# A two-layer streaming encoder step: two chunks of the first mixer's output read back in pieces through the ring of weight staging tiles

## The chip, the core and the metric

One core of one Trainium2 chip runs the whole program. The time is device microseconds of one launch. TensorE (PE, with its weight loads PEld), VectorE (DVE), ScalarE (ACT) and GpSimd (POOL) compute; SyncE (SP) only issues transfers, most of them on one hardware queue, in the order of the program. POOL issues the others, on a software queue.

## What is computed

Two layers on a prompt of 1024 frames and 8 streams of 16 frames (1152 tokens, width 1024). The part around the change is layer 0's mixer: stick-breaking attention (8 heads, in 4 pairs) beside a Conformer convolution, both joined and projected.

```python
def ab_mixer_prompt(h, w_in, w_out, dw_w, dw_b, ln_g, ln_b):
    q, k, v, u = ab_project(h, w_in)
    a_out = stick_breaking(q, k, v, ...)               # 512 columns: 4 pairs of heads
    c_out = conv_module(u_ext, dw_w, dw_b, ln_g, ln_b) # 512 columns
    out = jnp.concatenate([a_out, c_out], axis=-1) @ w_out
```

`x + out` then goes through an MLP, and so does layer 1 after its own attention.

## The kernel before, in words

Activations stand with channels on the 128 partitions: a chunk is 128 channels by 1152 tokens, and 1152 tokens are three groups `g` of `G` = 384. Products in full precision are done with every operand split into a high part and a rest (`split`, L182: ACT writes the high part at L185, DVE the rest at L186), three products each (`dense`, L211, matmuls at L225).

`mixer0` (L655) runs pair after pair, `p` = 0 to 3. While pair `p` attends (scores `z` L924 to L927, sigmoids L928 and L929, a running product on DVE L907 and L909, transposes `tpa` L388, products `ava` L398, result `cpa` L410), the projection of pair `p + 1` (`psp`) fills PE, and DVE does the taps of the convolution (`y`, `u`, L735). The samples' attention (`zs` L568, from cache tiles `ct`, which have 3 buffers) is merged in. `merge` and `level` set the order by given costs; a step's `after` and `lag` hold it back. Behind that, a scheduler places each engine's instructions, and every engine keeps that order.

The outputs of the pairs 0, 1 and 2 go to the scratch tensor `cat_d` in HBM (`cat_d<-cpa`, L363, on POOL's queue), because the tiles for them are those of the mixer's input `h`, which is read until the last projection. In the last pair (`p` = 3) the output projection starts with the three chunks that are done: `part_out` (L1069) multiplies chunks 0 to 2 by the weights `wo0a0` to `wo0a7`, into `psoa`. To that end `ready_chunks` (L1056) reads a chunk back into one tile `cr` of 128x1152 (its place is that of `sk`, the keys of the pair; there is one) and splits it into `cat` in three pieces. The names: `cr00` and `cr01` are chunks 0 and 1, `cr02` is chunk 2, which comes later; `cat0_00` and `cat0_01` are the high part and the rest of chunk 0, `cat0_10` and `cat0_11` of chunk 1. `expand` (L344) reads `sk` a last time at L351.

Weights come in through `staging` (L190): three tiles `st` of 128x512 in a ring; the split of one, on ACT and DVE, writes one of four tiles `hl` and gives the `st` tile free for the next transfer. A step's staged transfers come in the order in which the program asks for them.

```python
if p == 3:
    late, = ready_chunks(0, [2], pp, cat_t)
    late.name, late.after, late.lag = "ready", carry[-1].name, 3000.0
    fill[0].after, fill[0].lag = "ready", 5000.0
    fill = ready_chunks(0, range(2), pp, cat_t) + first + [late] + fill
```

Of the kernel before, what the change touches and what calls it, by code (L numbers as in the profile page):

```python
# [21 lines left out]
G = 384  # L22
NG = 3
# [17 lines left out]
def f(ap):  # L41
    return ap.bitcast(F32)
# [56 lines left out]
def run(steps):  # L99
    for s in steps:  # L100
        s.go()
# [23 lines left out]
def tile_trunk(ctx, tc, ins, outs):  # L125
# [8 lines left out]
    def pool(name):  # L134
        return tc.tile_pool(name=name, bufs=1, reuse_waits="tile")
# [7 lines left out]
    def bank(name):  # L143
        return psum.tile([P, 512], F32, tag="ps", name=name)
# [31 lines left out]
    cat_d = [dram.tile([KC, P, T], F32, name=f"cat_d{l}") for l in range(2)]  # L176
# [6 lines left out]
    def split(hi, lo, src):  # L183

        ACT(hi, src, AF.Copy)  # L185
        return tt(lo, src, f(hi), ALU.subtract)  # L186
# [3 lines left out]
    def staging(src, name, n=512):  # L190
        st = sp.tile([P, 512], F32, tag="st", name=f"st_{name}")
        dma(st[:, :n], src)
        return st
# [54 lines left out]
    chunks = {}  # L248
# [5 lines left out]
    def new_hs(name):  # L254
        return [[new_h(g, half, name) for half in range(2)] for g in range(NG)]
# [365 lines left out]
    def two_samples(a, b):  # L621

        (ka, sa, ta, pa), (kb, sb, tb, pb) = a, b
        if len(ta) == 1:
            return ka + sa + kb + ta + sb + pa + tb + pb
        return ka + sa + kb + ta[:1] + pa[:1] + ta[1:] + sb + pa[1:] + tb[:1] + pb[:1] + tb[1:] + pb[1:]
# [17 lines left out]
    def pipeline(jobs, carry):  # L644


        steps = []
        for first, second, tail in jobs:
            h = (len(carry) + 1) // 2
            steps += [first] + carry[:h] + [second] + carry[h:]  # L650
            carry = tail
        return steps, carry


    def mixer0():  # L655
        with ExitStack() as st:
# [8 lines left out]
            pp = Bufs(st.enter_context(pool("pair0")))  # L665
# [77 lines left out]
            def ag(c):  # L743
                return (chunk_steps(at[16 + c], got, ahead, h, ks, lambda ps, g: gate(c, ps, g), f"g{c}")
                        + chunk_steps(at[12 + c], got, ahead, h, ks, lambda ps, g: value(c, ps, g), f"a{c}"))
# [124 lines left out]
            def proj(p):  # L870
                steps = []
                for n, tag in enumerate(("sq", "sk", "sv")):
                    def evac(ps, g, n=n, tag=tag):
                        if g == 0:
                            S[tag, p] = pp.tile([P, T], F32, tag, f"{tag}0{p}")
                        if g < 2:
                            tt(S[tag, p][:, g * G:g * G + G], ps[:, :G], rstd[g], ALU.mult)
                        else:
                            ACT(S[tag, p][:, g * G:], ps[:, :G], AF.Copy)
                        if g == 2 and n:  # L880
                            put(outs["sb_k" if n == 1 else "sb_v"][p], S[tag, p])
                    steps += chunk_steps(at[4 * n + p], got, ahead, h, ks, evac, f"p{p}{n}")
                return steps

            def expand_qk(p):
                q, k = S["sq", p], S["sk", p]
                expand(qs, kd, kl, q, k)
                S["qn"] = pp.tile([P, P], F32, "qn", f"qn0{p}")
                S["kn"] = pp.tile([P, P], F32, "kn", f"kn0{p}")
                ACT(S["qn"], q[:, TP:], AF.Copy, scale=0.125)  # L890
                ACT(S["kn"], k[:, TP:], AF.Copy)
# [73 lines left out]
            carry, cat_t = [], None  # L965
            for p in range(4):
                S["p"] = p
                expand_qk(p)
                if p < 3:
                    fill = proj(p + 1)  # L970
                    if p < 2:
                        fill[10:10] = ag(p + 2)
                    n = TAPS[p + 1]
                    mix, now, taps = [], taps[:n], taps[n:]
                else:
                    cat_t = new_hs("cat0")
                    (first, fill), now = part_out(0, range(3), pp, cat_t), []
                    for s in taps:
                        s.pe = 900.0
                    mix = taps + conv_norm(lambda: (conv_pool.close(), Bufs(st.enter_context(pool("ln")), t1=3, yl=5))[1],  # L980
                                           cat_t)
                cat = Cat(0, p, wk, cat_t)
                jobs = attend(p, cat)
                body, left = pipeline(jobs[1:], jobs[0][2])
                steps = carry + [jobs[0][0]] + [Step(327.0, lambda p=p, g=g: expand_v(p, g)) for g in range(NG)]
                if p == 3:
                    late, = ready_chunks(0, [2], pp, cat_t)
                    late.name, late.after, late.lag = "ready", carry[-1].name, 3000.0
                    fill[0].after, fill[0].lag = "ready", 5000.0
                    fill = ready_chunks(0, range(2), pp, cat_t) + first + [late] + fill  # L990
                steps += [jobs[0][1]] + body
                carry = left
                if p == 3:
                    steps += carry
                cs = sample_out(cat, wk, p)
                load = sample_caches(0, p, cp)
                sample = two_samples(*(sample_steps(0, p, bg, S, wk, load, soft, cs) for bg in range(2)))
                run(level(merge(steps, sample, fill, mix), now))
            return cat_t

    def conv_norm(new_pool, cat_t):

        steps = []

        pools = []

        def norm(g):
            box = {}

            def load():  # L1010
                if g == 0:
                    pools.append(new_pool())
                box["y"] = [pools[0].tile([P, G], F32, "yl", f"yl{g}{c}") for c in range(4)]
                for c in range(4):
                    put(box["y"][c], cat_d[0][4 + c, :, g * G:g * G + G])

            def centre():
                yl = box["y"]
                mu = bank(f"mu{g}")
                for c in range(4):  # L1020
                    mm(mu[:, :G], ones, yl[c], start=c == 0, stop=c == 3)
                for c in range(4):
                    stt(yl[c], mu[:, :G], -1.0 / 512, yl[c], ALU.mult, ALU.add)

            def squares():
                yl, box["acc"] = box["y"], None
                for c in range(4):
                    box["acc"] = add_square(box["acc"], yl[c], pools[0], f"l{g}{c}")

            def scale():  # L1030
                box["r"] = pools[0].tile([P, G], F32, "r", f"rl{g}")
                diag, box["rows"], _ = rstd_of(box["r"], pools[0], box["acc"], 1.0 / 512, LN_EPS, f"l{g}")
                diag(box["acc"])

            def out(c):
                y = box["y"][c]
                tt(y, y, box["r"], ALU.mult)
                s = pools[0].tile([P, G], F32, "t1", f"ls{g}{c}")
                gg, bb = cvec[:, 1, c:c + 1], cvec[:, 2, c:c + 1]
                ACT(s, y, AF.Sigmoid, bias=bb, scale=gg)  # L1040
                ACT(y, y, AF.Identity, bias=bb, scale=gg)
                tt(y, y, s, ALU.mult)
                split(cat_t[g][1][0][:, c, :], cat_t[g][1][1][:, c, :], y)

            name = f"ln{g}"
            return ([Step(50.0, load, 0.0, f"l{name}"),
                     Step(2600.0, centre, 1900.0, f"c{name}", f"l{name}", 4000), Step(500.0, squares, 1400.0),
                     Step(700.0, scale, 1200.0, f"s{name}", f"c{name}", 5000),
                     Step(800.0, lambda: box["rows"](), 0.0, None, f"s{name}", 2500)]
                    + [Step(300.0, lambda c=c: out(c), 1500.0) for c in range(4)])  # L1050

        for g in range(NG):
            steps += norm(g)
        return steps

    def ready_chunks(layer, chunks, pp, cat_t):  # L1056

        steps = []
        for c in chunks:
            def go(c=c):  # L1060
                cr = pp.tile([P, T], F32, "sk", f"cr{layer}{c}")
                dma(cr, cat_d[layer][c])
                for g in range(NG):
                    hi, lo = (x[:, c % 4, :] for x in cat_t[g][c // 4])
                    split(hi, lo, cr[:, g * G:g * G + G])
            steps.append(Step(300.0, go))
        return steps
# [899 lines left out]
```

## Time and profile before

| what | value |
|---|---|
| median of 3 runs | 2749.17 us (2747.8 to 2751.32) |
| the profiled execution | 2750.03 us |
| its span, first to last instruction | 2748.2 us |
| PE busy | 2669.0 us (97%) |
| DVE busy | 2090.5 us (76%) |
| mean granted clock of PE | 0.991 |
| transfers of `cr` (10 in the program), issue to landing | 3.7 / 4.8 / 7.9 us (min, median, max) |
| the last pair of the first mixer, 425 to 548 us | PE busy 109.09 of 123.00 us |

The span is the program on the chip; the execution's time has 1.8 us more around it. A table like this tells which engine is full on the average; what one stage is worth is read in its own stretch of the trace, by what each engine waited for there.

### The profile page before, as it was taken

The page shows a single profiled execution, that of the slowest core. Times are in us where ns is not written, and L with a number is a line of the kernel's source. Part 1 is how long each engine was busy: PE and PEld are TensorE (multiplying, and loading weights), DVE is VectorE, ACT ScalarE, POOL GpSimd, SP SyncE. Part 2 cuts the span into 40 slices and gives each one's busy share as a digit, 9 for nine tenths or more (in the row PEclk, how much of TensorE's full clock was granted, in tenths as well). Part 3 has the DMA queues.
Part 4 walks back from the last instruction along what each step waited for, and adds up shares of the span by engine and source line. Part 5 has one row for each costly group of instructions (what it writes and reads, how often), then busy time and mean ns, then how long its engine had stood idle before and what let it go on. Part 6 is the DMA issues. An engine that isn't in the chain of part 4 may idle for free.

```text
span 2748.2 us, 50583 instructions
## 1 busy us (share of the span) xinstructions
PE 2669.0 (97%) x19362; PEld 2557.1 (93%) x19362; DVE 2090.5 (76%) x4117; ACT 1389.0 (51%) x2906; POOL 328.3 (12%) x599
## 2 busy tenths in 40 slices
PE   8999898999999999999999999998999999999998
PEld 8987776799999999999999999997999999999998
DVE  8999998888777755758577777778787777647577
ACT  5344456755554543435355555556555555434344
POOL 1100101041111100000011111110221111100001
PEclk9999999999999999999999999999999999999999
DMA  4434446454343377435444444446533343684344
GB/s 157 121 111 147 118 141 223 145 176 143 139 146 141 138 260 250 124 100 170 146 140 138 140 135 135 139 132 229 179 132 137 141 145 138 230 270 134 96 125 145
DMA packets 173203, 422.90 MB, mean 154 GB/s; under 512 B 25968, under 2 KB 53808, under 8 KB 170912
## 3 DMA queue, kind: packets, MB, share of 16 engines
q1 hardware_dynamic: 135696, 288.38, 33.1%
q0 software_dynamic: 37120, 131.27, 13.9%
q8 instruction: 152, 2.49, 0.4%
q14 instruction: 91, 0.75, 0.1%
q10 hardware_dynamic: 144, 0.02, 0.0%
HBM read 289.60 MB, written 117.34 MB: 148 GB/s over the span
## 4 chain that ended last, share of the span: by engine, by line
PE 76%; DVE 12%; ACT 4%; issue 4%; DMA 3%; POOL 0%; SPq 0%; DVEq 0%; ACTq 0%; POOLq 0%
PE um L1461 25%; PE pd L1686 25%; PE psc L225 10%; PE psp L225 3%; DVE y L735 3%; PE avc L467 2%; PE tpc L455 2%; DVE kp L907 2%; PE f L225 1%; PE psoa L225 1%; DMA cr<-cat_d 1%; PE zc L1201 1%; PE zc L1202 1%; PE zs L568 1%; PE so L602 1%
## 5 line engine op out<-in xcount | busy, mean ns | idle before, releaser
L225 PE MATMUL psc<-h,hl_wc 128*128 128x384 f32 x1728 | 327.2, 339 | 0.0
L225 PEld LDWEIGHTS psc<-h,hl_wc 128*128 128x128 f32 x1728 | 296.8, 188 | 13.3 <-issue 10.9
L1461 PE MATMUL um<-sl,hl_m 128*128 128x288 f32 x1548 | 240.3, 295 | 0.0
L1461 PEld LDWEIGHTS um<-sl,hl_m 128*128 128x128 f32 x1548 | 217.7, 188 | 0.0
L1686 PE MATMUL pd<-tm,hl_wd 128*128 128x288 f32 x1584 | 214.7, 294 | 0.0
L1686 PEld LDWEIGHTS pd<-tm,hl_wd 128*128 128x128 f32 x1584 | 211.3, 189 | 0.0
L735 DVE SCALAR_TENSOR_TENSOR y<-u,dw,y 128x1024 f32<-128x1024 f32 (+1 forms) x232 | 177.8, 806 | 0.6
L225 PE MATMUL psp<-h,hl_wi 128*128 128x384 f32 x864 | 165.7, 344 | 0.0
L1468 ACT ACTIVATE hdm<-hdm 128x288 f32<-128x288 f32 x192 | 84.7, 442 | 156.5 <-DVE hdm L1467 154.8
L225 PEld LDWEIGHTS psp<-h,hl_wi 128*128 128x128 f32 x864 | 150.9, 191 | 7.0 <-issue 6.2
L186 DVE TENSOR_TENSOR tm<-xr,tm 128x576 fp32r<-128x576 f32 (+1 forms) x120 | 85.8, 715 | 93.9 <-ACT tm L185 93.6
L185 ACT ACTIVATE tm<-xr 128x576 fp32r<-128x576 f32 (+1 forms) x120 | 77.6, 646 | 95.8 <-PE pd L1686 74.0
L1168 ACT ACTIVATE s<-s,mxc 128x640 f32<-128x640 f32 (+4 forms) x128 | 88.9, 694 | 60.2 <-DVE mxc L1165 58.6
L1461 PE MATMUL um<-sl,hl 128*128 128x288 f32 x756 | 119.1, 296 | 0.0
L1686 PE MATMUL pd<-th,hl_wd 128*128 128x288 f32 x792 | 113.7, 297 | 3.8 <-DVE th L186 3.7
L1686 PEld LDWEIGHTS pd<-th,hl_wd 128*128 128x128 f32 x792 | 108.2, 190 | 4.8 <-DVE th L186 4.2
L1686 PE MATMUL pd<-xr,hl_wd 128*128 128x288 f32 x792 | 112.4, 296 | 0.0
L1686 PEld LDWEIGHTS pd<-xr,hl_wd 128*128 128x128 f32 x792 | 108.0, 190 | 0.0
L1461 PEld LDWEIGHTS um<-sl,hl 128*128 128x128 f32 x756 | 106.4, 188 | 0.8
L1686 PE MATMUL pd<-tm,hl 128*128 128x288 f32 x768 | 104.9, 295 | 0.0
L1686 PEld LDWEIGHTS pd<-tm,hl 128*128 128x128 f32 x768 | 103.1, 188 | 0.0
L185 ACT ACTIVATE whc<-tpc 128x512 fp32r<-128x512 f32 (+1 forms) x144 | 72.5, 523 | 46.7 <-PE tpc L455 45.8
(526 smaller groups left out, 6637.0 us busy)
## 6 DMA issues: line engine op xcount, KB each, us to landing
xr<-hb_d SPq DMA_DIRECT2D x208, 288.0 KB, 3.0
xr<-in_w_up_dram SPq DMA_DIRECT2D x64, 512.0 KB, 4.2
hb_d<-hdm POOLq DMA_DIRECT2D x96, 288.0 KB, 2.4
hb_d<-t POOLq DMA_DIRECT2D x96, 288.0 KB, 2.4
wm<-in_w_down_dram SPq DMA_DIRECT2D x64, 256.0 KB, 4.0
st_wd<-in_w_down_dram SPq DMA_DIRECT2D x64, 256.0 KB, 3.5
st_wc<-in_w_in_c_dram SPq DMA_DIRECT2D x44, 256.0 KB, 2.9
xm_d<-xo POOLq DMA_DIRECT2D x16, 576.0 KB, 3.5
```

The lines of the kernel that those rows point to most:

```text
L185: ACT(hi, src, AF.Copy)
L186: return tt(lo, src, f(hi), ALU.subtract)
L225: mm(ps()[:, :G], hl[:, a, at:at + P], act[g][k // 4][b][:, k % 4, :], start=n == 0, stop=n == len(todo) - 1)
L455: nc.tensor.transpose(tp[:, c0 + q * P:c0 + (q + 1) * P], blocks.get(j, tile_q), ident)
L467: mm(st["av"][:, o0:o0 + n], vs[:, j, i].rearrange("p a d -> p (a d)"), src[:, c0:c0 + n], start=st["done"] == 0, stop=st["done"] == nmm - 1)
L568: mm(box["z"][at // 512][own, at % 512:at % 512 + kw], qb[:, own], k[:, b * kw:b * kw + kw], start=True, stop=True)
L735: stt(src if j == CW - 1 else dst, src, wj, dst, ALU.mult, ALU.add)
L907: nc.vector.tensor_tensor_scan(keep[:, 0:n][:, ::-1], keep[:, 0:n][:, ::-1], ones[:, 0:1].to_broadcast([P, n]), 1.0, ALU.mult, ALU.mult)
L1168: ACT(s[:, :n], s[:, :n], AF.Exp, bias=mx, scale=-1.0, accum_out=tot)
L1461: mm(banks[b, n][:, :TQ], w[:, a, c * P:c * P + P], combo(key, c)[:, h, n * TQ:n * TQ + TQ], start=k < 3 and c == 0 and i == 0, stop=c == ...
L1468: ACT(y, y, AF.Relu)
L1686: mm(ps, w[:, a, m * P:m * P + P], b[:, h, (n - ns[0]) * TQ:(n - ns[0]) * TQ + TQ], start=first and s == 0, stop=j == NJ - 1 and s == 2, s ...
```

## The change

Chunks 0 and 1 are no longer read whole into `cr`. A new function asks for each in three pieces of 128x384, each into a staging tile `st` (named `st_cr000` to `st_cr002` for chunk 0, `st_cr010` to `st_cr012` for chunk 1), and splits the piece from there. Chunk 2 comes as before. The calls stand at the same place of the program, ahead of the first weights of the output projection. Lines behind it are numbered 8 higher.

```diff
-                    fill = ready_chunks(0, range(2), pp, cat_t) + first + [late] + fill
+                    fill = ready_pieces(0, range(2), cat_t) + first + [late] + fill
...
+    def ready_pieces(layer, chunks, cat_t):
+
+        def go(c, g):
+            st = staging(cat_d[layer][c, :, g * G:g * G + G], f"cr{layer}{c}{g}", G)
+            split(*(x[:, c % 4, :] for x in cat_t[g][c // 4]), st[:, :G])
+
+        return [Step(100.0, lambda c=c, g=g: go(c, g)) for c in chunks for g in range(NG)]
```

How it moves instructions. SP's queue, from the last transfer that both have at the same place to the fourth tile of the last pair's sample keys (`ct03k03`), before:

```order
L537 DMA ct03k02_4520<-in_sb_k_dram 128x4x256
L1062 DMA cr00_4450<-cat_d0_109 128x1152
L1079 DMA xo00_4703<-in_x_dram 128x3x384
L192 DMA st_wo0a5_0_5125<-in_w_out_ab_dram 128x384
L192 DMA st_wo0a6_0_5297<-in_w_out_ab_dram 128x384
L1062 DMA cr01_4467<-cat_d0_109 128x1152
L537 DMA ct03k03_4533<-in_sb_k_dram 128x4x256
```

and with the change (`xo00` is the residual of the first output chunk):

```order
L1087 DMA xo00_4711<-in_x_dram 128x3x384
L192 DMA st_cr010_4471<-cat_d0_109 128x384
L192 DMA st_cr011_4477<-cat_d0_109 128x384
L192 DMA st_cr012_4481<-cat_d0_109 128x384
L192 DMA st_wo0a0_0_4485<-in_w_out_ab_dram 128x384
L192 DMA st_wo0a1_0_4490<-in_w_out_ab_dram 128x384
L192 DMA st_wo0a2_0_4730<-in_w_out_ab_dram 128x384
L192 DMA st_wo0a3_0_4820<-in_w_out_ab_dram 128x384
L192 DMA st_wo0a4_0_5000<-in_w_out_ab_dram 128x384
L192 DMA st_wo0a5_0_5133<-in_w_out_ab_dram 128x384
L192 DMA st_wo0a6_0_5305<-in_w_out_ab_dram 128x384
L537 DMA ct03k03_4541<-in_sb_k_dram 128x4x256
```

The three pieces of chunk 0 have taken the places that `wo0a0`, `wo0a1` and `wo0a2` had, far ahead of this stretch; the pieces of chunk 1 and seven weights now stand here, ahead of `ct03k03`.

DVE, from the last `cpa` of pair 2's second half to the end of the splits, before (`hl_wo0a2` and `hl_wo0a3` are weights; the splits of `hl_wo0a0` and `hl_wo0a1` stand much earlier, among the taps):

```order
L410 TENSOR_TENSOR cpa212_4417<-ava212_4408,ata212_4415 64x256
L186 TENSOR_TENSOR hl_wo0a2_0_4724<-st_wo0a2_0_4722,hl_wo0a2_0_4724 128x384
L186 TENSOR_TENSOR hl_wo0a3_0_4814<-st_wo0a3_0_4812,hl_wo0a3_0_4814 128x384
L186 TENSOR_TENSOR cat0_01_4453<-cr00_4450,cat0_00_4452 128x384 x3
L186 TENSOR_TENSOR cat0_11_4470<-cr01_4467,cat0_10_4469 128x384 x3
```

and with the change:

```order
L410 TENSOR_TENSOR cpa212_4417<-ava212_4408,ata212_4415 64x256
L186 TENSOR_TENSOR cat0_01_4439<-st_cr000_4436,cat0_00_4438 128x384
L186 TENSOR_TENSOR cat0_01_4439<-st_cr001_4456,cat0_00_4438 128x384
L186 TENSOR_TENSOR cat0_01_4439<-st_cr002_4460,cat0_00_4438 128x384
L186 TENSOR_TENSOR cat0_11_4474<-st_cr010_4471,cat0_10_4473 128x384
L186 TENSOR_TENSOR cat0_11_4474<-st_cr011_4477,cat0_10_4473 128x384
L186 TENSOR_TENSOR cat0_11_4474<-st_cr012_4481,cat0_10_4473 128x384
L186 TENSOR_TENSOR hl_wo0a0_0_4487<-st_wo0a0_0_4485,hl_wo0a0_0_4487 128x384
L186 TENSOR_TENSOR hl_wo0a1_0_4492<-st_wo0a1_0_4490,hl_wo0a1_0_4492 128x384
L186 TENSOR_TENSOR hl_wo0a2_0_4732<-st_wo0a2_0_4730,hl_wo0a2_0_4732 128x384
L186 TENSOR_TENSOR hl_wo0a3_0_4822<-st_wo0a3_0_4820,hl_wo0a3_0_4822 128x384
```

The four weights of the projection are now split behind both chunks.

PE, from the first product of the output projection (`psoa000`, first group), before (`tpa213` are transposes for the last quarter of pair 2):

```order
L225 MATMUL psoa000_4494<-cat0_00_4452,hl_wo0a0_0_4479 128x384
L388 MATMUL tpa2132_4501<-ident_69,sg216_4299 128x128
L388 MATMUL tpa2132_4501<-ident_69,sg217_4344 128x128
L388 MATMUL tpa2132_4501<-ident_69,sg216_4299 128x128
L388 MATMUL tpa2132_4501<-ident_69,sg217_4344 128x128
L225 MATMUL psoa000_4494<-cat0_01_4453,hl_wo0a0_0_4479 128x384
L225 MATMUL psoa000_4494<-cat0_00_4452,hl_wo0a0_0_4479 128x384
L388 MATMUL tpa2133_4508<-ident_69,sg216_4299 128x128
L388 MATMUL tpa2133_4508<-ident_69,sg217_4344 128x128 x2
L568 MATMUL zs0300_4514<-ct03k00_4516,qb0_124 32x256 x4
```

and with the change:

```order
L225 MATMUL psoa000_4502<-cat0_00_4438,hl_wo0a0_0_4487 128x384
L225 MATMUL psoa000_4502<-cat0_01_4439,hl_wo0a0_0_4487 128x384
L225 MATMUL psoa000_4502<-cat0_00_4438,hl_wo0a0_0_4487 128x384
L225 MATMUL psoa000_4502<-cat0_10_4473,hl_wo0a0_0_4487 128x384
L225 MATMUL psoa000_4502<-cat0_11_4474,hl_wo0a0_0_4487 128x384
L225 MATMUL psoa000_4502<-cat0_10_4473,hl_wo0a0_0_4487 128x384
L388 MATMUL tpa2132_4509<-ident_69,sg216_4299 128x128
L388 MATMUL tpa2132_4509<-ident_69,sg217_4344 128x128
L388 MATMUL tpa2132_4509<-ident_69,sg216_4299 128x128
L388 MATMUL tpa2132_4509<-ident_69,sg217_4344 128x128
L388 MATMUL tpa2133_4516<-ident_69,sg216_4299 128x128
L388 MATMUL tpa2133_4516<-ident_69,sg217_4344 128x128 x2
```

The products with chunk 1 have moved up next to those with chunk 0, and the transposes stand behind all six. What stands ahead of the first `psoa` and behind the twelfth to eighteenth is in the same order in both.

## Rows read from the trace of the kernel before

**Rows 1.** The head of the profile's page: span, and the shares of the chain that ended last.

```profile
span 2748.2 us, 50583 instructions
PE 76%; DVE 12%; ACT 4%; issue 4%; DMA 3%; POOL 0%; SPq 0%; DVEq 0%; ACTq 0%; POOLq 0%
```

**Rows 2.** The chain that ended last, in order of time, 400 to 560 us: start us, us, what.

```profile
421.99 1.54 DVE u L735 x2
423.56 1.23 DVE l L351
424.81 7.86 DMA cr<-cat_d
...
434.77 6.57 DMA cr<-cat_d
441.36 0.53 ACT cat L185
441.94 2.44 PE psoa L225 x12
...
452.08 4.01 DMA cr<-cat_d
```

**Rows 3.** PE's timeline: start us, us, engine, line, operation, tiles, shape, count, and in brackets the idle time before it with what ended it.

```profile
429.67 1.03 PE L388 MATMUL tpa<-ident,sg 128*128 128x128 f32 x6 [4.14 <-DVE sg L909]
433.27 0.69 PE L225 MATMUL psoa<-cat,hl_wo0a 128*128 128x384 f32 x1 [2.57 <-ACT cat L185]
...
438.33 2.85 PE L1021 MATMUL mu<-yl,ones 128*128 128x384 f32 x8
441.94 2.44 PE L225 MATMUL psoa<-cat,hl_wo0a 128*128 128x384 f32 x12 [0.76 <-ACT cat L185]
444.30 1.94 PE L398 MATMUL ava<-wa,vs 128*64 128x256 f32 x16
...
447.90 0.64 PE L568 MATMUL zs<-ct03k,qb 128*32 128x256 f32 x8
...
453.22 1.78 PE L225 MATMUL psoa<-cat,hl_wo0a 128*128 128x384 f32 x9
456.69 3.48 PE L225 MATMUL psoa<-cat,hl_wo0a 128*128 128x384 f32 x18 [1.68 <-ACT cat L185]
```

**Rows 4.** DVE's timeline, the same columns; the first four rows are from 380 to 400 us, the others from 408 to 470 us.

```profile
388.88 0.53 DVE L186 TENSOR_TENSOR hl_wo0a<-st_wo0a,hl_wo0a 128x384 fp32r<-128x384 f32 x1
389.33 1.35 DVE L909 TENSOR_TENSOR sgs<-sgs,kps 128x1151 f32<-128x1151 f32 x1
...
397.21 0.56 DVE L186 TENSOR_TENSOR hl_wo0a<-st_wo0a,hl_wo0a 128x384 fp32r<-128x384 f32 x1
397.69 1.21 DVE L351 TENSOR_TENSOR l<-sk,k 64x1024 fp32r<-64x1024 f32 x1
...
429.90 0.42 DVE L410 TENSOR_TENSOR cpa<-ava,ata 64x256 f32<-64x256 f32 x1
430.35 1.03 DVE L186 TENSOR_TENSOR hl_wo0a<-st_wo0a,hl_wo0a 128x384 fp32r<-128x384 f32 x2
433.25 1.50 DVE L186 TENSOR_TENSOR cat<-cr,cat 128x384 fp32r<-128x384 f32 x3 [1.87 <-ACT cat L185]
441.91 1.50 DVE L186 TENSOR_TENSOR cat<-cr,cat 128x384 fp32r<-128x384 f32 x3 [7.17 <-ACT cat L185]
```

**Rows 5.** ACT's timeline, the same columns.

```profile
418.38 0.53 ACT L185 ACTIVATE hl_wo0a<-st_wo0a 128x384 fp32r<-128x384 f32 x1 [0.54 <-PE psp L225]
419.08 1.05 ACT L348 ACTIVATE k<-sk 64x1024 fp32r<-64x1024 f32 x1 [0.17 <-PE z L924]
...
432.69 1.35 ACT L185 ACTIVATE cat<-cr 128x384 fp32r<-128x384 f32 x3 [1.84 <-DMA cr<-cat_d]
```

**Rows 6.** SP's timeline of issues: start us, us from the first to the last of the row.

```profile
366.53 0.89 SPq L192 DMA_DIRECT2D st_wo0a<-in_w_out_ab_dram  x2
...
430.94 0.86 SPq L192 DMA_DIRECT2D st_wo0a<-in_w_out_ab_dram  x2
434.77 0.33 SPq L1062 DMA_DIRECT2D cr<-cat_d  x1
437.16 11.81 SPq L537 DMA_DIRECT2D ct03k<-in_sb_k_dram  x4
```

**Rows 7.** Issue to landing. The first row is the tile view of `st_wo0a`, over its 8 transfers. The others are issues of short windows (count, KB of each, median us to landing), in this order: issued at 389 to 389.6 us, at 430.9 to 431.1 us, at 431.3 to 431.6 us, at 425.5 to 428 us, at 437 to 438 us, and the writes of `cat_d` at 401 to 422 us and at 446 to 449 us.

```profile
DMA to landing us min/median/max: 2.3/3.4/7.3
...
st_wo0a<-in_w_out_ab_dram SPq DMA_DIRECT2D x1, 192.0 KB, 3.1
...
st_wo0a<-in_w_out_ab_dram SPq DMA_DIRECT2D x1, 192.0 KB, 6.0
...
st_wo0a<-in_w_out_ab_dram SPq DMA_DIRECT2D x1, 192.0 KB, 7.3
...
xo<-in_x_dram SPq DMA_DIRECT2D x1, 576.0 KB, 10.2
...
ct03k<-in_sb_k_dram SPq DMA_DIRECT2D x1, 512.0 KB, 5.6
...
cat_d<-cpa POOLq DMA_DIRECT2D x2, 64.0 KB, 1.9
...
cat_d<-cpa POOLq DMA_DIRECT2D x1, 64.0 KB, 4.5
```

**Rows 8.** Stages: window, us, busy us (count) of PE, PEld, DVE, ACT and POOL, granted clock of PE, share and GB/s of the DMA engines.

```profile
380.00:390.00 10.00, 10.00 (x95) 8.67 (x94) 9.78 (x9) 7.15 (x19) 0.00 (x0) 1.00 0.01 2
390.00:400.00 10.00, 9.94 (x65) 8.47 (x64) 9.92 (x18) 6.26 (x15) 2.16 (x5) 1.00 0.68 236
...
430.00:433.00 3.00, 0.70 (x5) 0.30 (x3) 1.35 (x3) 0.91 (x2) 2.83 (x6) 0.54 1.03 364
433.00:436.00 3.00, 2.73 (x10) 2.25 (x10) 1.50 (x3) 2.12 (x5) 0.94 (x2) 0.50 1.07 393
436.00:442.00 6.00, 5.24 (x29) 2.34 (x28) 0.09 (x1) 1.73 (x4) 0.00 (x0) 0.91 0.99 350
```

## The prediction

> **What bounds the kernel now.** First the head of the page: PE holds 76% of the chain that ended last, transfers 3% [rows 1]. On the average there is nothing to win but PE time. The change, though, is one stretch of 20 us, so the second view is the chain by time, around 425 us [rows 2]. Up to 423.6 us DVE leads with the taps; then DVE's last read of `sk` (L351), and from 424.81 us the chain is a transfer of `cr` (7.86 us), its split, a second transfer of `cr` (6.57 us), its split, and the twelve products that waited for it. The reader sees two reads, one behind the other, through one tile.
>
> Third, PE's timeline there [rows 3]. PE waits 4.14 us for DVE's `sg`, which is not touched, then 2.57 us for chunk 0 (first `psoa` at 433.27 us) and 0.76 us for chunk 1. Between these two PE had other work: transposes, `zs`, `mu`. So what the reads cost is 3.3 us, not the 14 us that they hold of the chain. The chunk-1 wait ends at 441.94 us and `ava` starts at 444.30 us. If the first product came at a time T and nothing waited behind it, `ava` would start at T + 444.30 - 433.27 - 0.76 = T + 10.27 us. In other words: **the stretch is as long as before if T = 434.0 us** (433.27 + 0.76). Everything below is the search for T.
>
> **What the change removes, adds and moves.**
>
> *The transfers.* Two of 576 KB become six of 192 KB, four more issues on SP of some 0.4 us each [rows 6], in time in which SP waits anyway. The bytes are the same.
>
> *Chunk 0 early.* Its pieces take the places of the first three weights on SP's queue, of which two were issued at 366.53 us [rows 6]. They lie in `st` long before they are wanted. ACT can write the high part when the last projection has read `h` for the last time. It stands where the split of `wo0a2` stood, which ran at 418.38 us right after PE gave way [rows 5]. Three pieces take 1.35 us [rows 5] against 0.53 us, which delays the copy `k` at 419.08 us by some 0.5 us at most; DVE reads it at 423.56 us, so that hides it.
>
> *DVE among the taps.* Two weight splits leave it. The next instruction started 0.45 us after one and 0.48 us after the other [rows 4], in a stretch where DVE is busy 9.78 and 9.92 us of 10 [rows 8]. I take the whole 0.93 us as gained; the bounds are 0 and 0.93.
>
> *The wait that the change adds.* DVE writes chunk 0's rest only behind the last `cpa`, where before the weights' splits began at 430.35 us [rows 4]; now 429.42 us. Until then the three `st` tiles are held. Only then can the pieces of chunk 1 be asked for, and the weights `wo0a0` to `wo0a2` only when these have been split in turn. Before, the weights were in `hl` and one tile was read twice; now it is chunk 0, a round of transfers, a round of transfers, and the first product needs the second round. PE's queue keeps everything else behind that product: the transposes and `zs` that filled the time between the two waits stand behind it now.
>
> *T, step by step.* 429.42 + 0.5 (a third of the 1.50 us of three rests [rows 4]): the first `st` tile is free at 429.9 us and `cr010` is issued at 430.0. It lands after L1. From landing to the next issue: landing at 432.69, next issue at 434.77 with three pieces [rows 5, 6], so 2.08 us less two rests of 0.5, 1.06 us. `wo0a0` lands after L2. From landing to the first product: 441.36 to 441.94 [rows 2, 3], 0.58 us. T = 430.0 + L1 + 1.06 + L2 + 0.58 = 431.64 + L1 + L2. Against 434.03 the stretch is **longer by L1 + L2 - 2.39 us**.
>
> *L1 and L2.* For 192 KB the trace has 2.3 us at the least, 3.4 in the middle, 7.3 at the most [rows 7]. The two slow ones were asked for at 430.9 and 431.4 us, the very place: 6.0 and 7.3 us [rows 7]. But ahead of them on the queue stood `cr00` and `xo00`, which landed at 436.3 us (426.06 + 10.2 [rows 7]; its issue is the one behind `cr00`); they landed 0.6 and 2.4 us after that. Now `xo00` is first. I give it the 7.86 us that `cr00` took in that place [rows 2] from 425.1 us: 433.0 us. A piece 0.6 to 2.4 us behind lands at 433.6 to 435.4 us, that is L1 = 3.6 to 5.4; I take 4.2, nearer the lower end, because 576 KB less stand in the queue. For L2 I take the 3.1 us of 389 us [rows 7]: `ct03k03`, which before was asked for at 437.16 us [rows 6], is not in the queue yet. T = 438.9 us, and the stretch is longer by 7.3 - 2.39 = **4.9 us**. Bounds: 2.3 + 2.3 gives +2.2 us, 7.3 + 6.0 gives +10.9 us. No end is a gain: for that L1 + L2 would have to be under 2.39 us, and one of them alone has 2.3 us at the least.
>
> *What is queued behind.* `wo0a3` must wait for the tile of `wo0a0`: issue at T + 0.5, its high part split at T + 0.5 + 3.1 + 0.56 = T + 4.2 us. ACT's copies of the transposes stand behind it; `ava` wants them at T + 10.27 us: hidden. `ct03k03` stands behind `wo0a6`, which waits for the split of `wo0a3`: issue at T + 5.1 us, landing 5.6 us later [rows 7] at T + 10.7; PE wanted it at 447.90 us [rows 3], now T + 13.87. Covered by 3.2 us; it costs if the third round takes over 6.3 us.
>
> *The third chunk.* Its write and read (`cat_d<-cpa`, 4.5 us [rows 7], then `cr`, 4.01 us [rows 2]) hang on `ava` and shift with it; PE waits 1.68 us for it before and after [rows 3]. The write may meet less traffic, since sample keys stood beside it before; in a quiet place it took 1.9 us [rows 7]. So between 0 and 1.68 us come back; I take 0.5, near the row of the place itself.
>
> *PE's clock.* In 430 to 436 us the granted clock is 0.54 and 0.50, and 0.91 in 436 to 442: PE's low level, 1.2 of 2.4 GHz, up to some 437 us [rows 8], after the 4.14 us of waiting. So the first 3.8 us from 433.27 already run slow and lie in the 10.27 us. After T I take the same; ending earlier or later by that much gives or takes half of it, 1.9 us. The Trainium skill, "TensorE: Matmul & The Clock Gate", section "HAM oscillation — how this bites in real kernels", speaks against the change: a PE that waits for transfers is throttled and starts its next work cold. By that rule alone one would add the 1.9 us for the longer wait; by the rows nothing, since the clock is down there already.
>
> *Sum.* 4.9 - 0.5 = **+4.4 us**, and behind 460 us no engine has a source that does not shift along. The profiled execution would go from 2750.0 to 2754.4 us; the median shown is 0.86 us below that execution, so **2753.6 us** for it.
>
> **The rivals.** 0.2% of the time, 5.5 us, is about what a measurement of this kernel can tell from no change. The forecast lies just within.
>
> *Slower by more: both rounds meet a full queue.* Place: the pieces at 430 us and the weights some 5 us later. For it: the transfer share is 1.03 and 1.07 in 430 to 436 us [rows 8], and the two transfers asked for there took 6.0 and 7.3 us. Against it: 576 KB of them have left this time. With 6.0 and 4.5 us the stretch grows by 8.1 us, with the upper bounds by 10.9: 2757.3 to 2760. It decides from L1 + L2 = 8.4 us on (+6.0 less 0.5). The Trainium skill, "DMA: Bandwidth & Descriptors", section "Issuing engines are not separate DMA queues", says that what POOL asks for runs on the same engines and interleaves; the values and `yl` that POOL moves then would slow both rounds.
>
> *No change at all: short rounds and the third chunk's wait closed.* L1 + L2 = 5.5 and 1.68 us given back: +1.4 us, 2750.6 us. For it: half of the eight weight transfers took 3.4 us or less [rows 7]. Against it: those ran in quiet times.
>
> *Faster, as the change reads.* If the products did not wait for weights, PE would save 2.57 + 0.76 us and DVE's 0.93 us: -4.3 us, 2744.9 us; to pass 5.5 us the third chunk's wait must close too. Against it stands the order: the weights are asked for behind the chunks, through the same three tiles.
>
> **How the numbers follow.** Forecast 0.50, of which a fifth lies above 5.5 us; full queues 0.31; no change 0.13; faster 0.06, half of it by over 0.2%. So slower 0.10 + 0.31 = 0.41, faster 0.03, the same 0.56. The range, 2749.0 to 2759.5 us, holds the forecast with its clock term, no change, and most of the slower case; faster and the far upper end are left out. The forecast's own range is 2751 to 2756.
>
> **What would show it.** Step by step: the first `psoa` not at 433.3 but near 439 us, its wait put down to the split of `wo0a0`, some 9 us long with what DVE's part of it leaves; no wait of its own for chunk 1; `cr010` issued near 430.0 us; `cat` for chunk 0 on ACT near 418 us; `ava` near 449 us; `ct03k03` without a wait. Wrong would be: a first product before 434.5 us, weights asked for before 434 us, PE waiting for `ct03k03`, or a later stretch in which the shift is given back.

## The result, and the profile after the change

The change makes the kernel slower: 2759.03 us (median of 6 runs, 2755.76 to 2764.15) against 2751.06 us (6 runs), a ratio of 1.0032 [1.002, 1.0045], that is +8.8 us [+5.5, +12.4]; the two medians alone are 8.0 us apart. The forecast was +4.4 us, with 2753.6 us: the same direction and about half the size. Two further blocks of the unaltered change gave +8.2 us [+5.2, +11.3] and +7.2 us [+4.1, +9.9].

The profiled execution took 2764.15 us, span 2762.4 us. It already ran 4.95 us behind the first execution of the kernel before at 367 to 375 us, where both do the same. So times are best read as differences inside the stretch. PE's timeline, to be held against [rows 3]:

```profile
433.84 1.54 PE L388 MATMUL tpa<-ident,sg 128*128 128x128 f32 x6 [5.62 <-DVE sg L909]
444.18 2.29 PE L225 MATMUL psoa<-cat,hl_wo0a 128*128 128x384 f32 x6 [8.79 <-ACT hl_wo0a L185]
446.26 1.70 PE L388 MATMUL tpa<-ident,sg 128*128 128x128 f32 x7
...
450.75 2.85 PE L1021 MATMUL mu<-yl,ones 128*128 128x384 f32 x8
453.14 1.51 PE L225 MATMUL psoa<-cat,hl_wo0a 128*128 128x384 f32 x6
454.58 1.94 PE L398 MATMUL ava<-wa,vs 128*64 128x256 f32 x16
...
467.40 3.50 PE L225 MATMUL psoa<-cat,hl_wo0a 128*128 128x384 f32 x18 [1.93 <-ACT cat L185]
```

In place of two waits for chunks, 2.57 and 0.76 us, there is one, 8.79 us, and it is put down to the split of a weight. Behind it nothing waits up to `ava`. SP's issues and ACT's splits (to be held against [rows 5, 6]) show why:

```profile
430.23 0.37 SPq L1087 DMA_DIRECT2D xo<-in_x_dram  x1
435.11 1.61 SPq L192 DMA_DIRECT2D st_cr<-cat_d  x3
439.90 8.69 SPq L192 DMA_DIRECT2D st_wo0a<-in_w_out_ab_dram  x7
449.03 10.39 SPq L537 DMA_DIRECT2D ct03k<-in_sb_k_dram  x4
```

```profile
420.27 1.39 ACT L185 ACTIVATE cat<-st_cr 128x384 fp32r<-128x384 f32 x3
...
438.76 0.52 ACT L185 ACTIVATE cat<-st_cr 128x384 fp32r<-128x384 f32 x1 [2.69 <-DMA st_cr<-cat_d]
439.95 0.52 ACT L185 ACTIVATE cat<-st_cr 128x384 fp32r<-128x384 f32 x1 [0.67 <-DMA st_cr<-cat_d]
442.25 0.52 ACT L185 ACTIVATE cat<-st_cr 128x384 fp32r<-128x384 f32 x1 [1.77 <-DMA st_cr<-cat_d]
443.60 0.52 ACT L185 ACTIVATE hl_wo0a<-st_wo0a 128x384 fp32r<-128x384 f32 x1 [0.83 <-DMA st_wo0a<-in_w_out_ab_dram]
```

Two rounds one behind the other: pieces of chunk 1 asked for at 435.11, the first split at 438.76 (3.65 us), the first weight asked for at 439.90 (1.14 us later), split at 443.60 (3.70 us), first product 0.58 us after that. DVE, to be held against [rows 4]:

```profile
434.08 0.42 DVE L410 TENSOR_TENSOR cpa<-ava,ata 64x256 f32<-64x256 f32 x1
434.53 1.50 DVE L186 TENSOR_TENSOR cat<-st_cr,cat 128x384 fp32r<-128x384 f32 x3
439.32 0.56 DVE L186 TENSOR_TENSOR cat<-st_cr,cat 128x384 fp32r<-128x384 f32 x1 [3.30 <-ACT cat L185]
...
453.63 1.95 DVE L1023 SCALAR_TENSOR_TENSOR yl<-mu,yl 128x384 f32<-128x384 f32 x4 [5.40 <-PE mu L1021]
455.50 1.87 DVE L296 TENSOR_TENSOR sq_l<-sq_l,sq_l 128x384 f32<-128x384 f32 x3
457.40 0.42 DVE L410 TENSOR_TENSOR cpa<-ava,ata 64x256 f32<-64x256 f32 x1
```

The staging tiles come free with the rests at 434.53, right behind `cpa`. In the last three rows the last `cpa` of pair 2 starts the moment three `sq_l` have ended. In the kernel before it stood behind two of them and waited for ACT, with 0.36 us to spare; the third came behind it:

```profile
445.19 1.22 DVE L296 TENSOR_TENSOR sq_l<-sq_l,sq_l 128x384 f32<-128x384 f32 x2
446.77 0.42 DVE L410 TENSOR_TENSOR cpa<-ava,ata 64x256 f32<-64x256 f32 x1 [0.36 <-ACT ata L406]
447.22 0.56 DVE L296 TENSOR_TENSOR sq_l<-sq_l,sq_l 128x384 f32<-128x384 f32 x1
```

So DVE's order differs here too; the order lists above end ahead of this place. Every profile of the change has three squares ahead of that `cpa`, and both profiles of the kernel before have two.

The stages of the change, to be held against [rows 8] (columns as there):

```profile
434.00:440.00 6.00, 1.39 (x6) 0.98 (x6) 2.52 (x6) 1.76 (x4) 3.77 (x7) 0.50 1.01 327
440.00:444.00 4.00, 0.00 (x0) 0.00 (x0) 1.11 (x2) 1.40 (x3) 0.00 (x0) 0.50 0.71 256
444.00:449.00 5.00, 4.83 (x22) 3.51 (x22) 2.23 (x4) 2.59 (x6) 0.00 (x0) 0.50 0.52 156
449.00:455.00 6.00, 6.00 (x32) 3.95 (x34) 1.37 (x3) 1.33 (x3) 0.00 (x0) 1.00 0.69 204
```

The granted clock is at its low level through the wait and through the next 4.8 us of work.

**A measure for one stretch.** Below, M is the time between two writes on POOL's queue that every kernel here has: the last-but-one `cpa` of pair 2 and the last one. First the kernel before:

```profile
430.70 0.55 POOL L363 DMA_DIRECT2D cat_d<-cpa  x1
447.48 0.55 POOL L363 DMA_DIRECT2D cat_d<-cpa  x1 [13.54 <-DVE cpa L410]
```

then the change:

```profile
434.88 0.55 POOL L363 DMA_DIRECT2D cat_d<-cpa  x1
458.11 0.55 POOL L363 DMA_DIRECT2D cat_d<-cpa  x1 [20.00 <-DVE cpa L410]
```

M is 16.78 us before and 23.23 us in this execution: +6.45 us. A kernel's first write may itself come earlier; the change wins 0.78 us there (below). Each M is read from one profile. It repeats well for the kernel before (16.78 and 16.65 us) and for the change (23.23, 23.33 and 23.65 us), but one kernel below has 16.40 us in one execution and 14.48 us in another.

### The profile page after: what moved, and what is told of

It reads as the page before. It is cut to its first block, busy times and chain, and to the rows that moved or that the text cites. A ratio compares the mean times of both kernels' runs of the same rounds, so it can differ in the third digit from the quotient of the medians.

```text
span 2762.4 us, 50594 instructions
## 1 busy us (share of the span) xinstructions
PE 2674.7 (97%) x19362; PEld 2562.1 (93%) x19362; DVE 2090.9 (76%) x4117; ACT 1388.8 (50%) x2906; POOL 328.2 (12%) x599
## 4 chain that ended last, share of the span: by engine, by line
PE 70%; DVE 4%; ACT 2%; DMA 2%; issue 1%; DVEq 0%; ACTq 0%; SPq 0%
PE pd L1694 26%; PE um L1469 25%; PE psc L225 10%; PE avc L467 2%; PE tpc L455 2%; PE zc L1209 1%; PE zc L1210 1%; PE psoa L225 1%; DMA cr<-cat_d 1%; PE so L602 1%; PE zs L568 1%; DVE xr L1375 0%; PE psob L225 0%; ACT s L1176 0%; DMA xr<-in_w_up_dram 0%
```

## The experiments

Edits are against the changed kernel unless said. Theory A is the prediction's: two rounds of transfers ahead of the first product.

**The change once more.**

> The changed kernel once more, for a second profile. Measure M: from POOL's write of the last-but-one cpa of pair 2 to its write of the last one (16.8 us before, 23.2 us in the first profile of the change). Theory A (two rounds of transfers in the stretch, the rest is wander from execution to execution): M is again 22 to 24 us, the time 5 to 7 us over before, and the other shifts of the first profile (+2.1 us in the first 60 us, +1.4 at 235, +1.5 at 350, some +3.5 behind 530) come with other sizes or not at all. Theory B (the four additional issues and splits, or where the code now lies, cost time elsewhere as well): the same shifts at the same places, 8 to 14 us over before.

+8.2 us [+5.2, +11.3], M = 23.33 us. In this profile the early offset is gone (+0.47 us at 367 to 375 us in place of 4.95) and the stretch is the same, so the offset belongs to the execution and not to the change. In M and in the shifts theory A holds, and theory B's shifts at the same places did not come. The time is another matter: +8.2 us lies above theory A's 5 to 7 us, in theory B's 8 to 14, and the interval shuts out neither.

**The weights ahead of the pieces.**

```diff
-                    fill = ready_pieces(0, range(2), cat_t) + first + [late] + fill
+                    fill = first[:1] + ready_pieces(0, range(2), cat_t) + first[1:] + [late] + fill
```

> The weights wo0a0 and wo0a1 are asked for ahead of the pieces, the pieces still come through the staging tiles. Theory A (what cost time is that the weights stand behind two rounds of pieces): chunk 0 and its weights are there before PE wants them, chunk 1 takes one round which the transposes, zs and mu hide; M = 12 to 15 us, the time 3 to 6 us under before. Rival C (the pieces themselves cost: small transfers land late, four more splits): M stays over 17 us and the time at or over before.

M = 18.60 us, +1.4 us [-1.4, +4.1]: the first product does come early, but the forecast of a gain fails, and both numbers are those of rival C. PE's, SP's and ACT's timelines of this kernel:

```profile
425.67 0.42 PE L225 MATMUL psoa<-cat,hl_wo0a 128*128 128x384 f32 x1
...
438.87 0.69 PE L225 MATMUL psoa<-cat,hl_wo0a 128*128 128x384 f32 x1 [4.22 <-ACT cat L185]
```

```profile
426.95 0.44 SPq L537 DMA_DIRECT2D ct03k<-in_sb_k_dram  x1
431.35 2.21 SPq L192 DMA_DIRECT2D st_cr<-cat_d  x3
```

```profile
438.30 0.52 ACT L185 ACTIVATE cat<-st_cr 128x384 fp32r<-128x384 f32 x1 [3.00 <-DMA st_cr<-cat_d]
```

The wait has moved to chunk 1, whose first piece takes 6.95 us from issue to split (431.35 to 438.30) in place of 3.05 to 4.90 us in the change. With the weights gone from SP's queue, `ct03k03` (512 KB) is asked for ahead of it. A good part of the round that was taken out came back as a longer landing of the other. That `ct03k03` is the reason is read from the order and not tested.

**One round only: chunk 1 through `cr`.**

```diff
-                    fill = ready_pieces(0, range(2), cat_t) + first + [late] + fill
+                    fill = ready_pieces(0, [0], cat_t) + ready_chunks(0, [1], pp, cat_t) + first + [late] + fill
```

> Only chunk 0 comes in pieces; chunk 1 comes whole through the tile of sk as before. The weights still stand behind the pieces of chunk 0. Theory A: one round less than the change, so the first product comes about one landing and two splits (4 to 6 us) earlier than in the change: M = 17.5 to 19.5 us, the time 0 to 3 us over before. Rival C (pieces cost, by number): half of the excess of the change goes, M = 20.

M = 19.71 us, +3.3 us [+0.6, +6.1]: 3.6 us less than the change in M and 4.9 us in time. PE's first product:

```profile
437.46 1.01 PE L225 MATMUL psoa<-cat,hl_wo0a 128*128 128x384 f32 x2 [5.23 <-ACT hl_wo0a L185]
```

It waits 5.23 us for the weight, asked for at 431.96 us and split at 436.89. One round less, some 3.6 us less in M. But 19.71 us lies between theory A's upper end (19.5) and rival C's 20, so this run alone does not tell the two apart; the run with weights first and chunk 1 through `cr`, below, does.

**No round: chunk 0 in an idle tile** (from the kernel before; the taps' buffer is free by then, so both chunks can come early and the weights stay where they were).

```diff
-                    fill = ready_chunks(0, range(2), pp, cat_t) + first + [late] + fill
+                    early = cv.tile([P, UW], F32, "u", "cr00")[:, :T]
+                    dma(early, cat_d[0][0])
...
+                    fill = [Step(300.0, first_chunk)] + ready_chunks(0, [1], pp, cat_t) + first + [late] + fill
```

> The kernel before, but chunk 0 is read whole into a tile of the convolution that has been idle since some 320 us, so that chunk 1 need not wait for chunk 0's split; nothing goes through the staging tiles. Theory A: both waits for chunks (2.57 and 0.76 us) go, and PE can do a first product and zs while it waits 4.1 us for DVE: M = 12 to 15 us, 3 to 6 us under before. If the reads were hidden anyway: same time as before, M = 16 to 17.

M = 16.40 us, -2.2 us [-4.7, +0.6]. M is that of the expectation's other line (16 to 17 us), and a gain of 3 to 6 us isn't shown. The wait for chunk 1 did not go: chunk 1 was asked for 10 us earlier than before (424.69 us), but needed 9 us to be split (433.76), and PE still waited for it:

```profile
434.34 0.69 PE L225 MATMUL psoa<-cat,hl_wo0a 128*128 128x384 f32 x1 [2.27 <-ACT cat L185]
```

**The same a second time.**

> The kernel with chunk 0 in an idle tile, a second time: 16.40 us between the puts and -2.2 us (-4.7 to +0.5) the first time. By the stretch alone: 16 to 17 us and -1.5 to +1 us. If the first time's gain holds: -4 to -2 us.

M = 14.48 us, under the 16 to 17 us that were expected, and -0.8 us [-3.3, +1.7]. Here chunk 1 was waited for 1.02 us. The kernel's time is the lowest in both blocks, but neither block tells it from the kernel before.

**Weights first, chunk 1 through `cr`.**

```diff
+                    fill = (first[:1] + ready_pieces(0, [0], cat_t) + ready_chunks(0, [1], pp, cat_t)
+                            + first[1:] + [late] + fill)
```

> Weights first, chunk 0 in pieces through the staging tiles, chunk 1 whole through the tile of sk. Theory A (pieces cost nothing by themselves; only what stands behind them in the ring does): as e4, M = 16 to 17 us, the time 0 to 4 us under before. Rival C (pieces cost): M over 17.5.

M = 16.35 us as expected, and 0.0 us [-2.8, +2.8], the upper end of what was expected. PE's first products:

```profile
424.06 0.42 PE L225 MATMUL psoa<-cat,hl_wo0a 128*128 128x384 f32 x1
...
431.56 0.69 PE L225 MATMUL psoa<-cat,hl_wo0a 128*128 128x384 f32 x1 [0.57 <-ACT cat L185]
```

No weight is waited for, and chunk 1 costs 0.57 us of waiting. Chunk 0 through the staging tiles shows no cost, in M or in time, so long as the first product waits for no weight and chunk 1 does not come through the same tiles behind it. For chunk 0 that speaks against rival C: the one-round kernel has the same pieces and differs only in the place of the weights, and its M was 19.71 us.

**Sixteen idle products ahead of the first one** (the idle-tile kernel; PE multiplies chunk 0's high part with itself into a spare bank, 9 times ahead of the wait for `sg` and 7 times behind it, so that the first products don't meet a low clock; the results are never read).

> As e4, with 16 products of 128x384 on PE that nothing reads, between the transposes for which PE waits: they are additional work and only keep PE busy in its wait for DVE. Theory D (in e2 and e4 the waits that went were eaten by PE's low clock: it was low for 6 us of work in each): the clock is up when the output projection begins, the low stretch is under 2 us, M = 13.5 to 15 us and the time 3 to 6 us under before. Rival: the clock does not matter and chunk 1's landing at 433 us sets the end: M = 16 to 17, the time as e4.

M = 14.65 us as expected, but +4.1 us [+1.4, +6.9] in time, where a gain was expected. The second time, beside the idle tile alone:

> The kernel with chunk 0 in an idle tile and 16 idle products, a second time. The first time its stretch was 2.1 us shorter than that of the kernel before (14.65 against 16.78 us between the two puts) and its time 4.1 us longer, with a mean granted clock of 0.9899 over 12 runs against 0.9918 of the kernel before on that chip. Theory A (chance): the clock of these runs is that of the kernel before within 0.0005 and the time -3 to +1 us. Theory B (the low clock elsewhere belongs to the kernel): between the puts 14 to 15 us again, the mean clock 0.001 to 0.002 lower, the time +3 to +6 us.

M = 14.89 us and +3.3 us [+0.6, +5.8]. The mean granted clock of the runs was 0.9907 against 0.9912: within theory A's bound, while the time fits theory B. So by these numbers some 2 us are won in the stretch against the kernel before and 5 to 6 us lost outside it, twice. Both profiles fall back in several steps of 1 to 2 us behind 460 us, but single executions do so anyway: between DVE's instructions at 470 us and the last ones these two lose 4.4 and 3.4 us against the first execution of before, the kernel with the weights first, which has no idle products, loses 4.8, and the third execution of the change gains 1.2. The cause is not settled. Nor do the idle products win anything sure in M over the idle tile alone, which had 16.40 and, in this block, 14.48 us.

**The kernel before, once more.**

> The kernel before once more, for a second profile: what differs between two executions of one program. Theory A: M is 16.5 to 17.0 us again; outside of that stretch the starts differ by up to 2 us at places where PE waits, as they did between the two profiles of the change.

M = 16.65 us, one run of 2754.51 us. But the wander that the expectation allowed, 2 us, is exceeded: the execution is 1.18 us ahead of the first one at 338 us and 3.11 us behind it at 367 us (on DVE and on POOL's write). Two stages of the kernel before in each of its two profiles (columns as in [rows 8]), first the execution that the prediction read:

```profile
307.00:311.00 4.00, 4.00 (x44) 3.30 (x43) 3.94 (x6) 0.98 (x2) 0.53 (x1) 0.57 0.18 28
334.00:342.00 8.00, 5.49 (x44) 4.30 (x45) 7.86 (x11) 2.46 (x5) 1.63 (x3) 1.00 0.42 123
```

then the second:

```profile
307.00:311.00 4.00, 4.00 (x48) 3.71 (x37) 3.94 (x7) 1.14 (x4) 0.53 (x1) 1.00 0.64 197
334.00:342.00 8.00, 6.67 (x31) 6.11 (x31) 7.86 (x12) 1.47 (x3) 1.64 (x3) 0.57 0.42 108
```

The same program has its clock low at 307 us in one execution and at 334 us in the other. Such stretches move single executions by some us, which is why a stretch is judged here by M and not by where it lies.

**The change with 32 idle products**, 9 behind the first transpose and 23 behind the next three, in the two waits that PE has anyway.

```diff
+                    def warm():
+                        spare = bank("warm")
+                        hi = cat_t[0][0][0][:, 0, :]
+                        for n in range(32):
+                            mm(spare[:, :G], hi[:, :P], hi, start=True, stop=True)
...
+                    fill = (ready_pieces(0, [0], cat_t) + [Step(0.0, warm)] + ready_pieces(0, [1], cat_t)
+                            + first + [late] + fill)
```

> The change with 32 idle products (of chunk 0 with itself, into a spare bank, never read) on PE in the two waits ahead of the first product of the output projection: 9 behind the first transpose, 23 behind the next three. In the change PE does 4.5 us of work at the low clock after its first product at 439.9 us. Theory A (that work is what the low clock costs): with PE busy up to some 3 us before that product the clock is up, 2.2 us come back, and the time between the two puts of pair 2 on POOL, 23.2 to 23.3 us in the change, falls to 20.5 to 22; the time falls with it, 2 to 3 us under the change, +5 to +7 against the kernel before. Theory B (what is won in the stretch is lost at a low clock elsewhere, as the warmed kernel before this seemed to show, 2.1 us won and 4.1 lost): the same 20.5 to 22, but the time stays at the change's, +7 to +11, and the mean granted clock of the runs is no higher than the change's.

M = 20.81 us, as both theories had it, and +8.0 us [+5.0, +11.3] where the change beside it had +7.2: theory B's time. PE's timeline, then its stages:

```profile
430.46 6.21 PE L994 MATMUL warm<-cat 128*128 128x384 f32 x23
436.51 0.60 PE L388 MATMUL tpa<-ident,sg 128*128 128x128 f32 x4
439.97 0.62 PE L225 MATMUL psoa<-cat,hl_wo0a 128*128 128x384 f32 x2 [2.86 <-ACT hl_wo0a L185]
...
448.22 1.94 PE L398 MATMUL ava<-wa,vs 128*64 128x256 f32 x16
```

```profile
430.00:435.00 5.00, 5.00 (x18) 5.00 (x19) 2.03 (x5) 0.79 (x2) 3.77 (x7) 0.52 0.99 324
435.00:440.00 5.00, 2.14 (x15) 1.87 (x13) 1.72 (x4) 2.47 (x6) 0.00 (x0) 1.00 0.75 270
440.00:444.00 4.00, 4.00 (x31) 3.06 (x35) 1.88 (x4) 2.31 (x5) 0.00 (x0) 1.00 0.59 161
```

The clock is up before the first product, and from that to `ava` are 8.25 us in place of 10.33 to 10.40. So the low clock costs the change 2.1 us in its stretch. In the time the 2.1 us don't show. Against the change beside it the intervals are too wide to say that they were lost. Against the kernel before something is: up to the third chunk this execution is 2.96 us later (its offset of 1.01 us taken off), which is under the whole interval. Theory B is not met either, for its mean clock was to be no higher than the change's, and it is (0.9913; the change 0.9901, before 0.9912). Where the time goes is open; the profiled execution is the fastest of its six.

**The change a third time**, beside the last three on one chip.

> The change unaltered, beside the three others on one chip. Theory (the stretch and little more): 22.5 to 24 us between the puts, +5.5 to +9 us. Rival (more is lost behind the stretch): +9 to +12 us with the same stretch. In both the mean granted clock is 0.001 to 0.002 under that of the kernel before, since the clock is low for 17 us of the stretch and not for 6.8.

M = 23.65 us, +7.2 us [+4.1, +9.9]; mean granted clock 0.9901 against 0.9912. All three numbers are those of the theory of the stretch and little more; the interval alone does not shut out the rival's range.

## Why the prediction was right in its mechanism and too small in its size

The table takes from each profile of the change its own offset ahead of the taps (+4.95, +0.47 and -0.81 us on POOL's writes at 367 to 375 us), so that every entry is a time later than in the kernel before.

| step | forecast | first | second | third |
|---|---|---|---|---|
| DVE's gain among the taps | -0.93 | -0.78 | -0.79 | -0.78 |
| L1 + L2 | 4.2 + 3.1 = 7.3 | 3.65 + 3.70 = 7.35 | 3.05 + 4.46 = 7.51 | 4.90 + 2.91 = 7.81 |
| landing to the next issue | 1.06 | 1.14 | 1.14 | 1.14 |
| first product against 434.03 | +4.9 | +5.20 | +5.36 | +5.66 |
| first product to `ava` | 10.27 | 10.40 | 10.33 | 10.36 |
| `ava` to the last write (before 3.18) | no change | 3.53 | 3.53 | 3.53 |
| last write | +4.9 | +5.68 | +5.77 | +6.10 |
| third chunk on PE | +4.4 | +5.76 | +5.36 | +6.13 |

**Right.** The wait of the first product, 8.8 to 9.3 us long and put down to the weight; no wait of its own for chunk 1; `cr010` asked for near 430.0 us (430.16 to 430.17 with the offset taken off); chunk 0 on ACT early (415.3 us likewise, some 3 us before the forecast's 418); `ava` near 449 us (449.6 to 450.1 likewise); `ct03k03` without a wait. L1 + L2 came out at 7.35 to 7.81 us where 7.3 was taken, although the two terms changed places from execution to execution. So the rival with full queues (8.4 us and more) didn't happen. That the time fell in its range (2757.3 to 2760 us) is luck: the two rounds did not bring it there.

**PE's clock.** The rows said that a longer wait adds nothing, since the clock is down already; from first product to `ava` it took 0.06 to 0.13 us more, and with the clock brought up 2.1 us less. The Trainium skill, "TensorE: Matmul & The Clock Gate", section "HAM oscillation — how this bites in real kernels", has PE start its work cold behind such a wait; the runs agree on that (granted clock 0.50 for the 4.8 us of work behind it), but they show no further 1.9 us for a longer wait.

**Too small, term by term.** DVE's gain by 0.15 us (0.33 and 0.46 us for the two splits that left; the bounds held it). The step from landing to the next issue by 0.08. L1 + L2 by up to 0.5. A term was missed: 0.35 us from `ava` to the last write. It is not that DVE came later to its work there: `yl` starts 0.97 us before `ava` in the kernel before and 0.95 us before it in the change. But one more square `sq_l` stands ahead of `cpa` in DVE's order, so that the squares end at 457.37 us and `cpa` starts at 457.40, where before it waited 0.36 us for ACT. The prediction followed PE's queue and ACT's behind the wait, and not DVE's. Last, the third chunk was to give back 0.5 us: the stretch grew by 0.08 us there in the first profile, gave back 0.41 in the second and grew by 0.03 in the third. Its write landed in 4.1, 4.4 and 4.2 us against 4.5 before, and PE waited 1.93, 1.45 and 1.89 us against 1.68: in two of three executions nothing came back.

**The step that failed** is the prediction's sum, "4.9 - 0.5", with its close that behind 460 us no engine has a source that does not shift along. Three of its terms were mis-sized: the 0.5 us that the third chunk was to give back (measured: nothing in two executions, 0.41 in one), the way from `ava` to the last write, put at nothing (0.35 us), and L1 + L2 (7.3 taken, 7.35 to 7.81 measured); with the small differences named above they bring +5.4 to +6.1 us at the third chunk in place of +4.4. But +7.2 to +8.8 us were measured. The rest, some 2 us, lies within each interval (their lower ends are +4.1, +5.2 and +5.5), yet all three points stand on one side; weighted by their widths they give some +8.0 us [+6.2, +9.8] (an estimate), just clear of the stretch. So the close of the sum is probably wrong too, and its cause stays open. It was not found in the profiles: from the third chunk to the end the three executions of the change move by +3.5, +1.0 and -0.7 us against the first execution of before, and the second execution of before by +1.4 us. Nor is more low clock behind the stretch shown: the clock is low for 17.1 us of the stretch in each profile of the change and for 6.8 us in both of the kernel before, which would lower the mean by 0.0019 (an estimate: half of 10.2 us in 2750), and the runs of the two later blocks have it lower by 0.0015 and 0.0011.

**What the experiments say of the cause.** One round out: 3.6 us less in M, 4.9 us less in time. Both out (weights first, chunk 1 through `cr`): no difference from before. Weights first with all pieces: a longer landing in place of the round. That the two rounds through three tiles cost the 5 to 6 us of the stretch is shown; the 2 us beyond it are not explained by them. That reading chunk 0 early is worth something is not shown: PE waits for `sg` in any case, and behind it comes chunk 1.

## What to carry to other kernels

Where two kinds of data go through one ring of tiles, the second waits for the last reader of the first. Count the rounds of issue, landing and split that lie ahead of the first consumer, and price them with the landing times of that very place: that gave 7.3 us for 7.35 to 7.81. Then compare every engine's order behind the new wait, not only that of the engine that waits, and take no gain for a wait that "may" shrink. To judge a change of a few us in a program of some ms, measure between two events inside the stretch; whole executions differ by more.

## What was not expected of the hardware

**Part of the low clock is at other places in each execution.** In all five profiles of the kernel before and of the change it is low at four places near 215 to 220, 512 to 524, 611 to 625 and 1864 to 1876 us. At other places, such as near 307, 334 and 976 us, it is low in some of the five only. What PE did just ahead does not tell them apart: from 304 to 307 us it was busy for 1.36 of 3 us in the first execution of before and for 1.40 in the second, and only in the first did the clock fall. Of 82 executions of the kernel before, the median time is 2756.7 us for the 12 whose mean granted clock was 0.990, 2752.8 us at 0.991 (28), 2751.4 us at 0.992 (21) and 2748.6 us at 0.993 (14). One stage of the change in its first and in its third profile (executions of 2764.15 and 2754.61 us) shows one of the sites:

```profile
2032.00:2040.00 8.00, 7.71 (x36) 7.72 (x37) 7.65 (x31) 4.22 (x9) 0.00 (x0) 0.57 0.47 138
```

```profile
2032.00:2040.00 8.00, 7.96 (x52) 6.94 (x52) 6.61 (x27) 4.54 (x11) 0.57 (x1) 1.00 0.53 170
```

PE is busy nearly throughout in both, at a granted clock of 0.57 in one and 1.00 in the other. The counts (36 and 52 products) can't be compared: the first execution is 7.6 us behind the third there, so the same microseconds hold other instructions.

**A stretch won need not show in the time.** In the change the idle products took 2.4 to 2.8 us out of M (20.81 against 23.23, 23.33 and 23.65), and the time beside it was +8.0 in place of +7.2 us. The kernel with the idle tile took 4 us longer with idle products than without them, side by side (+3.3 and -0.8 us). Why is open.

**A landing goes with what stands ahead of it.** The same 192 KB from `cat_d` took 3.05 to 4.90 us from issue to split with `xo00` the last ahead of them on SP's queue (three executions), and 6.95 us with `ct03k03` in between (one). That the queue is the reason is likely and was not tested alone.
